# The two middle column groups of an output projection, computed as one pair of seven block products

## The chip, the cores and the metric

The kernel runs on one core of a Trainium2 chip. The metric is the device time of one execution, in microseconds (us); lower is better. Engines are named as in the profile: PE is TensorE (matmuls; PEld are its weight loads), DVE is VectorE, ACT is ScalarE, POOL is GpSimd and SP is SyncE, which here only issues transfers.

## The reference

Two layers of a decoder trunk, 512 tokens by 2048 channels in float32. Each layer normalises its input, projects it to 6656 columns, runs three token mixers on parts of these (retention with 6 heads, differential attention with 4 heads, a gated linear recurrence, called LRU, on 768 channels), joins their gated outputs to 2048 channels, and sends these through one output projection:

```python
mixed = jnp.concatenate([ret_out, diff_out, lru_out], axis=-1)
y = jnp.einsum('bse,ed->bsd', mixed, w_out[l])
x = x + rms_norm(y, post_norm_g[l])
```

The change concerns the second of these lines: a product of a 512x2048 matrix (`mixed`) with a 2048x2048 matrix (`w_out`), once for each layer.

## The kernel before

**Precision.** Each float32 operand of a projection is split in two parts, `hi` (rounded to the type fp32r) and `lo` (what is left), and each product is made of three matmuls: hi by hi, hi by lo and lo by hi (L204). Weights are split when they are loaded: ScalarE writes `whi` (L164), VectorE subtracts it from the raw weights and writes `wlo` (L165). Activations are split where they are produced; for the output projection these are 16 pairs `mhi`, `mlo` of 128 channels by 512 tokens.

**Tiling.** All weights come in chunks of 256 rows by 512 columns (`raw`, 512 KB, two k-tiles of 128 rows). There are three buffers each of `raw`, `whi` and `wlo`. A `Pass` (L89) is one column group of 512 columns: 8 chunks, all 16 k-tiles. `run_pass` (L191) runs over chunks and, in a chunk, over up to four accumulators of 128x512 in PSUM (`big`, four banks). In form B, that of the output projection, the accumulators are the four blocks of 128 tokens, the activations are the stationary operand and 512 columns of weights move. The last two chunks are done bank after bank, so that the banks end one after the other; each bank's `evac` follows when its last matmul is issued.

**The output projection** is four column groups (L899 to L902). The fourth is done in two halves of two token blocks. The order of k-tiles is LRU, retention, differential attention (`outk`, L851), as the mixers end. `evac_y` (L794) takes the sum of squares of a result on ScalarE (L797) and multiplies by the gain of the norm on VectorE (L804); after the fourth group, `finish` (L820) scales, adds the residual, stores, and for layer 0 also transposes and splits the input of layer 1.

**Order of the work.** Loads are asked for by `ensure` (L168) two chunks ahead of the matmuls. The smaller work of the mixers is written as generators in a queue `side`, of which `pump` (L177) advances one step after each second group of matmuls; `drain` empties it before the output projection (L971). Instructions on PE, DVE, ACT and POOL are put in order at build time by a planner with priorities: loads, weight splits and `evac` have a bonus of 300 instructions (`HP`, L43). SP is left in program order (`manual_schedule`, L100), so a transfer that waits for its buffer holds up those behind it. Almost all tiles of 128x512 come from one pool `up` of 77 buffers (`NU`, L37): a new tile waits until a buffer is free. The residual's input tiles `xr` are loaded by `load_x` (L777), started before the third group (L976), two at each step; `finish` needs those of two token blocks after each half of the fourth group.

Of the kernel before, what the change touches and what calls it, by code (L numbers as in the profile page):

```python
# [23 lines left out]
P = 128  # L24
DM = 2048
S = 512
# [11 lines left out]
WBUFS = 3  # L38
NWARM = 9
# [6 lines left out]
C_RQ, C_RV, C_RG, C_DQ, C_DK, C_DV, C_DG, C_LX = 0, 1536, 2304, 3072, 3584, 4096, 4608, 5120  # L46

# [41 lines left out]
class Pass:  # L89
    def __init__(self, form, wsrc, kts, banks, act, evac, defer=False):  # L90
        self.form, self.wsrc, self.kts = form, wsrc, kts
        self.banks, self.act, self.evac, self.defer = banks, act, evac, defer


@with_exitstack
def tile_hybrid_trunk(ctx, tc, x, xt, pos, ppar, lamqk, w_in, gw, w_out, postg, cp, cm, out):
# [54 lines left out]
    loaded = [0]  # L151
    last_copy = [None]

    def load_chunk(i):
        p, c = chunk_list[i]
        raw = wp.tile([P, 2, S], F32, tag="raw", name=nm("raw"))
        hi = wp.tile([P, 2, S], F32R, tag="whi", name=nm("whi"))
        lo = wp.tile([P, 2, S], F32R, tag="wlo", name=nm("wlo"))
        src = p.wsrc[c].rearrange("p (k c) -> p k c", k=2)
        for a, b in (((0, 1), (1, 2)) if i == 0 else ((0, 2),)):  # L160
            if i == 0:
                load_xt(a)
            nc.sync.dma_start(raw[:, a:b, :], src[:, a:b, :])
            last_copy[0] = A.copy(hi[:, a:b, :], raw[:, a:b, :])  # L164
            V.tensor_tensor(lo[:, a:b, :], raw[:, a:b, :], hi[:, a:b, :], op=ALU.subtract)  # L165
# [19 lines left out]
    def drain():  # L185
        while side:
            pump()
# [3 lines left out]
    def run_pass(p):  # L191
# [39 lines left out]
        for c in range(nch):  # L231
            del chunk_tiles[base + c]

# [334 lines left out]
    def diff_final(l, st):  # L568
# [3 lines left out]
        for h in range(DIFF_H):  # L572
            ps = SM("dT")
            for tb in range(NT):
                T.transpose(ps[:, tb * P:(tb + 1) * P], st["dod"][tb][:, h * P:(h + 1) * P], ident)
            hi, lo = U("mhi", F32R), U("mlo", F32R)
            A.activation(hi, ps, AF.Identity, scale=subg[:, l:l + 1])
            V.scalar_tensor_tensor(lo, ps, subg[:, l:l + 1], hi, op0=ALU.mult, op1=ALU.subtract)
            st["mix"][6 + h] = (hi, lo)
            yield  # L580
# [85 lines left out]
    def lru_final(st):  # L666
# [8 lines left out]
        for t in range(LRU_T):  # L675
# [7 lines left out]
            st["mix"][10 + t] = (hi, lo)  # L683
# [56 lines left out]
    def ret_final(st, heads):  # L740
        for h in heads:
# [8 lines left out]
            st["mix"][h] = (hi, lo)  # L750
# [26 lines left out]
    def load_x(l, st):  # L777
        src = x2 if l == 0 else xs
        for tb in range(NT):
            for n in range(4):  # L780
# [3 lines left out]
                if n % 2:  # L784
                    yield
# [8 lines left out]
    def evac_y(l, st, n):  # L794
        def f(tb, ps):
            y = U("y")
            A.activation(junk, ps, AF.Square, accum_out=ssy[:, tb, n:n + 1])  # L797
            st["y"][tb, n] = y
# [5 lines left out]
            V.tensor_tensor(y, ps, st["pg"][n], op=ALU.mult)  # L804
            if n == 2:
# [36 lines left out]
    def new_state():  # L842
        return {k: {} for k in ("h", "dq", "dk", "dqs", "dks", "dv", "dg", "lx", "lg", "lh", "rq", "rk", "rv", "rg", "ro",
                                "mix", "y", "ry", "xr", "pg")} | {"turned": None}
# [6 lines left out]
    outk = list(range(10, 16)) + list(range(0, 10))  # L851
    layer_passes = []
    for l in range(DEPTH):
# [45 lines left out]
        for n in range(4):  # L899
            groups = [tbs] if n < 3 else [[0, 1], [2, 3]]  # L900
            for g in groups:
                seq.append((Pass("B", WO[n], outk, g, st["mix"], evac_y(l, st, n)), []))  # L902
        layer_passes.append(seq)
        for p, _ in seq:
            passes.append(p)
            for c in range(len(p.kts) // 2):
                chunk_list.append((p, c))
# [55 lines left out]
    for l in range(DEPTH):  # L963
# [5 lines left out]
        for i, (p, tasks) in enumerate(layer_passes[l]):  # L969
            if i == 13:  # L970
                drain()  # L971
            if i in (13, 14, 15, 16):
                n = i - 13
# [104 lines left out]
```

## Time and profile before

| | |
|---|---|
| time, median of 3 runs | 1637.45 us (1636.26 to 1637.54) |
| profiled execution | 1638.29 us |
| its span, first to last instruction | 1636.5 us |
| granted TensorE clock | 0.998 |
| PE busy | 1624.9 us, 99% |
| DVE busy | 928.4 us, 57% |
| ACT busy | 646.3 us, 39% |
| POOL busy | 60.1 us, 4% |
| HBM read, written | 167.86 MB, 8.39 MB; 108 GB/s over the span |

The profile is one execution; its time is compared with its own span, and medians with medians. A group of instructions is named by its line, engine, operation, output and inputs (`big<-whi,mhi` is a matmul of the output projection), the count, and then busy time and the mean duration of one in ns. Matmuls are pipelined: the next begins before the one before has ended, so the distance between starts, and not the duration, tells what one costs. "Idle before" is the engine's idle time just ahead of the group's instructions, with what ended it.

### The profile page before, as it was taken

What the parts mean: (1) busy time and instruction counts of PE and PEld (TensorE: products, weight loads), DVE (VectorE), ACT (ScalarE), POOL (GpSimd) and SP (SyncE); (2) the same over time, 40 slices, a digit from 0 to 9 for tenths busy, and PEclk for the clock granted to TensorE, in tenths of its full rate; (3) what the DMA queues carried; (4) which work ended last, traced back from release to release, by engine and by line L of the source; (5) the groups of instructions that cost most, each with busy time, mean ns of one, the idle gap of its engine ahead of it and who ended that gap; (6) DMA issues with size and microseconds to landing.
All of it is one profiled execution on the core that took longest, in us unless ns stands there. A gap on an engine that the chain in (4) does not pass through costs nothing.

```text
span 1636.5 us, 19326 instructions
## 1 busy us (share of the span) xinstructions
PE 1624.9 (99%) x7541; PEld 1344.5 (82%) x7541; DVE 928.4 (57%) x1558; ACT 646.3 (39%) x1014; POOL 60.1 (4%) x84
## 2 busy tenths in 40 slices
PE   9999999999999999999999999999999999999997
PEld 7888888888788888888888888887888888888886
DVE  7657756556586555233762774645857644442336
ACT  7243334346742223222752343435673222332232
POOL 1010000000000000000120000000000000000001
PEclk9999999999999999999999999999999999999999
DMA  6423331323233222354643223222323322233635
GB/s 229 124 86 108 97 96 59 98 78 98 79 102 95 79 72 85 109 173 137 217 155 103 91 91 102 65 85 79 100 87 91 102 65 78 90 99 107 204 124 199
DMA packets 54747, 177.50 MB, mean 108 GB/s; under 512 B 6656, under 2 KB 7680, under 8 KB 54656
## 3 DMA queue, kind: packets, MB, share of 16 engines
q1 hardware_dynamic: 52592, 169.94, 32.4%
q0 software_dynamic: 1920, 6.29, 1.1%
q8 instruction: 59, 0.97, 0.2%
q14 instruction: 32, 0.26, 0.1%
q10 hardware_dynamic: 144, 0.04, 0.0%
HBM read 167.86 MB, written 8.39 MB: 108 GB/s over the span
## 4 chain that ended last, share of the span: by engine, by line
PE 83%; issue 14%; DVE 1%; ACT 1%; DMA 0%; POOL 0%; POOLq 0%; DVEq 0%; ACTq 0%
PE big L209 75%; PE gate L622 1%; PE acc L515 1%; PE rs L691 1%; PE ro L716 1%; PE sc L482 1%; PE sc L483 1%; DVE wlo L165 1%; PE wT L505 1%; PE ro L719 0%; PE kv L705 0%; PE hT L831 0%; DVE y L823 0%; DMA raw<-in_w_out 0%; ACT whi L164 0%
## 5 line engine op out<-in xcount | busy, mean ns | idle before, releaser
L165 DVE TENSOR_TENSOR wlo<-raw,whi 128x1024 fp32r<-128x1024 f32 (+1 forms) x289 | 351.3, 1219 | 440.7 <-ACT whi L164 423.1
L164 ACT CAST whi<-raw 128x1024 fp32r<-128x1024 f32 (+1 forms) x289 | 302.4, 1048 | 590.9 <-PE big L209 477.1
L209 PE MATMUL big<-hhi,whi 128*128 128x512 f32 x1024 | 401.8, 393 | 0.0
L209 PE MATMUL big<-hhi,wlo 128*128 128x512 f32 x1024 | 399.1, 390 | 0.0
L209 PE MATMUL big<-hlo,whi 128*128 128x512 f32 x1024 | 399.0, 390 | 0.0
L209 PE MATMUL big<-whi,hhi 128*128 128x512 f32 x640 | 254.4, 400 | 0.0
L209 PE MATMUL big<-whi,hlo 128*128 128x512 f32 x640 | 250.8, 392 | 0.0
L209 PE MATMUL big<-wlo,hhi 128*128 128x512 f32 x640 | 250.2, 392 | 0.0
L209 PEld LDWEIGHTS big<-hhi,wlo 128*128 128x128 f32 x1024 | 192.2, 188 | 40.6
L209 PEld LDWEIGHTS big<-hhi,whi 128*128 128x128 f32 x1024 | 192.4, 188 | 39.5
L209 PEld LDWEIGHTS big<-hlo,whi 128*128 128x128 f32 x1024 | 192.4, 188 | 38.7
L209 PE MATMUL big<-whi,mhi 128*128 128x512 f32 x512 | 199.9, 390 | 0.4 <-ACT whi L164 0.4
L209 PE MATMUL big<-wlo,mhi 128*128 128x512 f32 x512 | 199.4, 390 | 0.5 <-DVE wlo L165 0.5
L209 PE MATMUL big<-whi,mlo 128*128 128x512 f32 x512 | 199.8, 390 | 0.0
L209 PEld LDWEIGHTS big<-wlo,hhi 128*128 128x128 f32 x640 | 120.7, 189 | 26.0
L209 PEld LDWEIGHTS big<-whi,hhi 128*128 128x128 f32 x640 | 121.0, 189 | 24.3 <-ACT whi L164 0.8
L209 PEld LDWEIGHTS big<-whi,hlo 128*128 128x128 f32 x640 | 120.9, 189 | 23.7
L209 PEld LDWEIGHTS big<-wlo,mhi 128*128 128x128 f32 x512 | 96.1, 188 | 20.8 <-DVE wlo L165 1.0
L209 PEld LDWEIGHTS big<-whi,mhi 128*128 128x128 f32 x512 | 96.1, 188 | 20.6 <-ACT whi L164 0.9
L209 PEld LDWEIGHTS big<-whi,mlo 128*128 128x128 f32 x512 | 96.1, 188 | 19.6
L491 ACT ACTIVATE pr<-sc,mx 128x128 f32<-128x128 f32 (+3 forms) x64 | 33.2, 523 | 86.7 <-DVE mx L488 86.7
L417 DVE TENSOR_TENSOR rt<-qk,sin_d 32x512 f32<-32x512 f32 x64 | 43.7, 683 | 3.5 <-ACT qk L459 2.5
(212 smaller groups left out, 1333.1 us busy)
## 6 DMA issues: line engine op xcount, KB each, us to landing
raw<-in_w_in SPq DMA_DIRECT2D x207, 512.0 KB, 3.6
raw<-in_w_out SPq DMA_DIRECT2D x80, 512.0 KB, 3.4
xT<-in_xt SPq DMA_DIRECT2D x16, 256.0 KB, 6.6
xr<-in_x SPq DMA_DIRECT2D x16, 256.0 KB, 6.5
xs<-y POOLq DMA_DIRECT2D x16, 256.0 KB, 3.6
xr<-xs SPq DMA_DIRECT2D x16, 256.0 KB, 5.6
pg<-in_postg SPq DMA_DIRECT2D x8, 256.0 KB, 3.8
out<-y POOLq DMA_DIRECT2D x8, 256.0 KB, 5.9
```

The lines of the kernel that those rows point to most:

```text
L164: last_copy[0] = A.copy(hi[:, a:b, :], raw[:, a:b, :])
L165: V.tensor_tensor(lo[:, a:b, :], raw[:, a:b, :], hi[:, a:b, :], op=ALU.subtract)
L209: T.matmul(ps[b], lhsT=lhsT, rhs=rhs, start=(cnt[b] == 0), stop=(cnt[b] == total - 1))
L417: V.tensor_tensor(t2[b:b + w, :], raw[a:a + w, :], sin[a:a + w, :], op=ALU.mult)
L482: T.matmul(ps[:, :n], lhsT=qs[:, blk], rhs=ks[:, :n], start=True, stop=False)
L483: T.matmul(ps[:, :n], lhsT=qs[:, blk], rhs=kl[:, :n], start=False, stop=True)
L491: A.activation(p[:, :n], sc[c][:, :n], AF.Exp, bias=mx[:, c:c + 1], scale=0.125, accum_out=sums[:, h:h + 1])
L505: T.transpose(ps[:, kb * P:(kb + 1) * P], w[:, kb * P:(kb + 1) * P], ident)
L515: T.matmul(accs[i][:, h * P:(h + 1) * P], lhsT=wt[:, kb * P:(kb + 1) * P], rhs=dv[kb][:, h * P:(h + 1) * P], start=(kb == 0), stop=(kb == i))
L622: T.matmul(ps[:BW, :], lhsT=wt[:BW, cols], rhs=at[:BW, :], start=(n == 0), stop=(n == 2))
L691: T.matmul(ps[:, n * P:(n + 1) * P], lhsT=k[:, n * P:(n + 1) * P], rhs=q[:, n * P:(n + 1) * P], start=True, stop=True)
L716: T.matmul(po[:, n * P:(n + 1) * P], lhsT=sT[:, n * P:(n + 1) * P], rhs=v[:, n * P:(n + 1) * P], start=True, stop=(n == 0))
```

## The change

The first and the fourth column group stay plain. The second and the third become one `Pair`, a product of block matrices two by two: the activations are halved by tokens (256 and 256) and by channels (k-tiles 0 to 7 and 8 to 15), the weights by channels and by columns (512 and 512). In place of eight block products seven are made, of sums and differences of blocks (Winograd's form). One product is a 256x1024 by 1024x512 matrix product: four units, one for each weight chunk, of 12 matmuls (two token blocks, two k-tiles, three matmuls). The order of units is A11 B11 alone, and then three couples that alternate unit by unit: S1 T1 with S3 T3, S2 T2 with S4 B22, A12 B21 with A22 T4. A unit keeps two accumulators open for four units, so a couple fills the four banks.

- **Sums of activations** (S1 to S4): the class `Sums` makes them on VectorE while the first group runs, and splits them in hi and lo; they stay in the pool `up`. The splits of the fourth are made later, from the second S1 unit on. It works on unsplit activations `mf`, which `diff_final` and `ret_final` now copy from PSUM with one more ScalarE instruction each (ten a layer); for LRU they are put together again as hi + lo. All activations are also renumbered so that k-tiles 0 to 5 are LRU's (`K_LRU`, `K_RET`, `K_DIFF`); the order of the weight rows was this before.
- **Sums of weights** (T1, T2, T4) are made on VectorE in a tile pair `x` in `up`, to which the chunk just loaded is added; T3 is made by a transfer from POOL's queue that adds the second chunk to a loaded one (`accum_op`). Chunks of the lower right block are so read twice.
- **Loading in three steps**: `ensure` now loads a pair's chunk four units before it is split, adds two units before, and splits as before. Plain chunks are loaded and split at the last step.
- **Results**: products A11 B11, S1 T1 and S3 T3 are copied from PSUM to `up` by ScalarE (`held`); the others are combined with these by VectorE. The squares and the gain are then taken from SBUF, in place. The mean square is closed when the three first groups of a token block are there, whichever ends last.
- `load_x` is started at the first unit of A12 B21 and loads one tile for each step.

```diff
+A11_B11, A12_B21, S1_T1, S2_T2, S4_B22, S3_T3, A22_T4 = range(7)
+SUM_OF = {S1_T1: 0, S2_T2: 1, S3_T3: 2, S4_B22: 3}
+UNITS = [(A11_B11, c) for c in range(4)] + [
+    (s, c) for both in ((S1_T1, S3_T3), (S2_T2, S4_B22), (A12_B21, A22_T4)) for c in range(4) for s in both]
...
+    def load_unit(i):
+        p, (s, c) = chunk_list[i]
+        w1, w2 = p.w
+        if s == A11_B11:
+            src = p.x[c] = [U("wx"), U("wx")]
+            for kk in range(2):
+                nc.sync.dma_start(src[kk], w1[c][:, kk * S:(kk + 1) * S])
+        elif s == S1_T1:
+            p.kept[c] = load_raw(w2[c])
+        elif s == S2_T2:
+            p.kept[c] = load_raw(w2[c + 4])
+        elif s == A12_B21:
+            p.kept[c] = load_raw(w1[c + 4])
+        yield
+        if s in (S1_T1, S2_T2, A22_T4):
+            src = p.x[c]
+            for kk in range(2):
+                V.tensor_tensor(src[kk], src[kk], p.kept[c][:, kk, :], op=ALU.add)
+        elif s != A11_B11:
+            src = p.kept[c]
+        if s == S3_T3:
+            nc.gpsimd.dma_start(src, w2[c + 4].rearrange("p (k c) -> p k c", k=2), accum_op=ALU.add)
+        yield
+        hi, lo = split_tiles()
+        if isinstance(src, list):
+            for kk in range(2):
+                split(hi[:, kk, :], lo[:, kk, :], src[kk])
+        else:
+            split(hi, lo, src)
+        chunk_tiles[i] = (hi, lo)
+        yield
     def ensure(i):
-        while loaded[0] <= min(i, len(chunk_list) - 1):
-            with tc.high_priority(HP):
-                load_chunk(loaded[0])
-            loaded[0] += 1
+        for step, more in enumerate((LOAD, ADD, 0)):
+            while loaded[step] <= min(i + more, len(chunk_list) - 1):
+                n = loaded[step]
+                if n not in steps:
+                    steps[n] = (load_unit if isinstance(chunk_list[n][0], Pair) else load_chunk)(n)
+                with tc.high_priority(HP):
+                    next(steps[n])
+                loaded[step] += 1
...
+    def run_pair(p, begin):
...
+        def evac(s, t, x):
+            o1, o2 = p.out
+            if s in (A11_B11, S1_T1, S3_T3):
+                held = {A11_B11: p1, S1_T1: p5, S3_T3: p7}[s]
+                held[t] = U("held")
+                A.copy(held[t], x)
+            elif s == A12_B21:
+                e = U("e")
+                V.tensor_tensor(e, x, p1[t], op=ALU.add)
+                o1(t, e)
+            elif s == S2_T2:
+                w, e = U("w"), U("e")
+                V.tensor_tensor(w, x, p1[t], op=ALU.subtract)
+                V.tensor_tensor(p5[t], p5[t], w, op=ALU.add)
+                V.tensor_tensor(e, p5[t], p7[t], op=ALU.subtract)
+                V.tensor_tensor(p7[t], p7[t], w, op=ALU.subtract)
+                o2(2 + t, e)
+            elif s == S4_B22:
+                V.tensor_tensor(p5[t], x, p5[t], op=ALU.add)
+                o2(t, p5.pop(t))
+            else:
+                V.tensor_tensor(p7[t], x, p7[t], op=ALU.add)
+                o1(2 + t, p7.pop(t))
+
+        for n, (s, c) in enumerate(UNITS):
+            if (s, c) in begin:
+                side.append(begin[s, c]())
+            if s in SUM_OF:
+                until(lambda: (SUM_OF[s], c) in p.sums.parts)
+            ensure(base + n + 2)
+            hi, lo = chunk_tiles.pop(base + n)
+            for t in range(2):
+                if c == 0:
+                    ps[s, t] = pb.tile([P, S], F32, tag="big", name=nm("big"))
+                for kk in range(2):
+                    ah, al = (stationary(s, c, kk, part)[:, t * P:(t + 1) * P] for part in range(2))
+                    for m, (wt, at) in enumerate(((hi, ah), (hi, al), (lo, ah))):
+                        T.matmul(ps[s, t], lhsT=at, rhs=wt[:, kk, :], start=(c == kk == m == 0),
+                                 stop=(c == 3 and kk == 1 and m == 2))
+                if c == 3:
+                    with tc.high_priority(HP):
+                        evac(s, t, ps.pop((s, t)))
+            pump()
+    class Sums:
...
+        def make(self, c):
+            f, plain = self.f, self.plain
+            for k in (2 * c, 2 * c + 1):
+                if k not in f:
+                    f[k] = U("mf")
+                    hi, lo = self.act[k]
+                    V.tensor_tensor(f[k], hi.bitcast(F32), lo.bitcast(F32), op=ALU.add)
+            yield
+            last = None
+            for n in (0, 2, 1, 3):
+                t = plain[n, c] = U("sf")
+                for kk in range(2):
...
+                    V.tensor_tensor(t[:, cols], a, b, op=ALU.subtract)
+                if last is not None:
+                    self.split(last, c)
+                last = n
+                if n in (2, 1):
+                    yield
...
+            m = st["mf"][K_RET + h] = U("mf")
+            A.copy(m, ps)
...
-        for n in range(4):
-            groups = [tbs] if n < 3 else [[0, 1], [2, 3]]
-            for g in groups:
-                seq.append((Pass("B", WO[n], outk, g, st["mix"], evac_y(l, st, n)), []))
+        st["sums"] = Sums(st["mf"], st["mix"])
+        seq.append((Pass("B", WO[0], allk, tbs, st["mix"], out_y(l, st, 0)), []))
+        seq.append((Pair(WO[1], WO[2], st["mix"], st["sums"], out_y(l, st, 1), out_y(l, st, 2)), []))
+        for g in ([0, 1], [2, 3]):
+            seq.append((Pass("B", WO[3], allk, g, st["mix"], out_y(l, st, 3)), []))
...
-            if i == 15:
-                side.append(load_x(l, st))
-            run_pass(p)
+            if isinstance(p, Pair):
+                run_pair(p, {(S1_T1, 1): st["sums"].rest, (A12_B21, 0): lambda l=l, st=st: load_x(l, st)})
+            else:
+                run_pass(p)
```

More of the change, by code (lines that the diff above doesn't have):

```diff
@@ L38 @@
 WBUFS = 3
+ADD, LOAD = 2, 4
 NWARM = 9
@@ L150, in tile_hybrid_trunk, with load_raw, split_tiles, split @@
     chunk_tiles = {}
-    loaded = [0]
+    steps = {}
+    loaded = [0, 0, 0]
     last_copy = [None]
+    def load_raw(src):
+        raw = wp.tile([P, 2, S], F32, tag="raw", name=nm("raw"))
+        nc.sync.dma_start(raw, src.rearrange("p (k c) -> p k c", k=2))
+        return raw
+    def split_tiles():
+        return (wp.tile([P, 2, S], F32R, tag="whi", name=nm("whi")),
+                wp.tile([P, 2, S], F32R, tag="wlo", name=nm("wlo")))
+    def split(hi, lo, raw):
+        last_copy[0] = A.copy(hi, raw)
+        V.tensor_tensor(lo, raw, hi, op=ALU.subtract)
@@ L154, in load_chunk @@
     def load_chunk(i):
         p, c = chunk_list[i]
[L156 to L161, printed above, removed]
+        yield
+        yield
+        if i:
+            raw = load_raw(p.wsrc[c])
+            hi, lo = split_tiles()
+            split(hi, lo, raw)
+        else:
+            src = p.wsrc[0].rearrange("p (k c) -> p k c", k=2)
+            raw = wp.tile([P, 2, S], F32, tag="raw", name=nm("raw"))
+            hi, lo = split_tiles()
+            for a in range(2):
@@ L186, in drain, with until @@
         while side:
+            pump()
+    def until(done):
+        while not done():
+            assert side
             pump()
@@ L792, in squares, with out_y, f @@
                     yield
[L794 to L798, printed above, removed]
+    def out_y(l, st, n):
+        def f(tb, src):
+            A.activation(junk, src, AF.Square, accum_out=ssy[:, tb, n:n + 1])
+            y = st["y"][tb, n] = U("y") if n in (0, 3) else src
             if n == 3:
@@ L803, in f @@
                 G.tensor_tensor(st["ry"][tb], ms, mhalf[:, :1], op=ALU.pow)
-            V.tensor_tensor(y, ps, st["pg"][n], op=ALU.mult)
-            if n == 2:
+            V.tensor_tensor(y, src, st["pg"][n], op=ALU.mult)
+            if n < 3 and all((tb, m) in st["y"] for m in range(3)):
                 ss = tiny("sy", 1)
@@ L905, in tile_hybrid_trunk @@
             passes.append(p)
-            for c in range(len(p.kts) // 2):
-                chunk_list.append((p, c))
+            for u in UNITS if isinstance(p, Pair) else range(len(p.kts) // 2):
+                chunk_list.append((p, u))
     st = states[0]
@@ L971, in tile_hybrid_trunk @@
                 drain()
-            if i in (13, 14, 15, 16):
-                n = i - 13
+                side.append(st["sums"].all())
+            for n in {13: (0,), 14: (1, 2), 15: (3,)}.get(i, ()):
                 st["pg"][n] = U("pg")
                 nc.sync.dma_start(st["pg"][n], postg[l, n * S:(n + 1) * S].partition_broadcast(P))
-            if i == 15:
-                side.append(load_x(l, st))
-            run_pass(p)
+            if isinstance(p, Pair):
+                run_pair(p, {(S1_T1, 1): st["sums"].rest, (A12_B21, 0): lambda l=l, st=st: load_x(l, st)})
+            else:
+                run_pass(p)
             for t in tasks:
```

60 lines of the change are left out of this document (50 added, 10 removed).

## The prediction, made before the changed kernel was run

> **What bounds the kernel now.** First the page: busy time by engine, the costliest groups and the issues.
>
> ```profile
> PE 1624.9 (99%) x7541; PEld 1344.5 (82%) x7541; DVE 928.4 (57%) x1558; ACT 646.3 (39%) x1014; POOL 60.1 (4%) x84
> ...
> L209 PE MATMUL big<-whi,mhi 128*128 128x512 f32 x512 | 199.9, 390 | 0.4 <-ACT whi L164 0.4
> ...
> raw<-in_w_out SPq DMA_DIRECT2D x80, 512.0 KB, 3.4
> ...
> out<-y POOLq DMA_DIRECT2D x8, 256.0 KB, 5.9
> ```
>
> TensorE is busy for 99% of the span. The group is one of three of the output projections (512 each, 1536 in all), and it waited 0.4 us in the whole run. A duration of 390 ns is no price, because matmuls overlap; that comes from the chain of waits, which merges runs of matmuls without a gap:
>
> ```profile
> 1.39 4.02 PE warm L953 x9
> ...
> 643.42 145.34 PE big L209 x641
> ```
>
> 145.34 / 641 = 0.2267 us for each matmul, through nearly the whole output projection of layer 0. The stages (engine sums over windows that I laid at 192 x 0.2267 = 43.5 us; columns: PE, PEld, DVE, ACT, POOL busy, granted clock, DMA share, GB/s) are the first, second and third column group, the fourth's first half, then the second and third of layer 1:
>
> ```profile
> 641.10:684.60 43.50, 43.50 (x197) 36.00 (x196) 14.50 (x15) 13.39 (x19) 0.00 (x0) 1.00 0.30 99
> 684.60:728.10 43.50, 43.50 (x194) 36.02 (x193) 12.54 (x13) 11.06 (x17) 0.00 (x0) 1.00 0.49 151
> 728.10:771.60 43.50, 43.50 (x194) 36.02 (x193) 13.20 (x19) 11.06 (x17) 0.00 (x0) 1.00 0.45 151
> 771.60:793.40 21.80, 21.59 (x98) 17.65 (x97) 12.32 (x16) 9.26 (x12) 1.82 (x3) 1.00 0.57 181
> 1495.10:1538.70 43.60, 43.60 (x194) 36.12 (x193) 12.65 (x13) 11.16 (x17) 0.00 (x0) 1.00 0.46 151
> 1538.70:1582.20 43.50, 43.50 (x194) 36.02 (x193) 12.98 (x18) 11.06 (x17) 0.00 (x0) 1.00 0.45 152
> ```
>
> In the stages that the change rewrites, TensorE has no gap at full clock, VectorE is used for 30%, ScalarE for 25%, the DMA engines for under half. A matmul less is worth its 0.2267 us there, as long as the idle engines can carry what replaces it.
>
> **The change, part by part.** *Matmuls removed.* Two plain groups take 2 groups x 16 k-tiles x 4 token blocks x 3 = 384 matmuls in each layer. The pair takes 28 units x 2 halves x 2 k-tiles x 3 = 336, of the same form (a 128x128 stationary, 512 columns moving). 48 less in each layer, 96 in all: 96 x 0.2267 = **21.8 us**. The pair has 336 x 0.2267 = 76.2 us in each layer, a unit of 12 matmuls 2.72 us.
>
> *Work added on VectorE and ScalarE.* Prices come from these groups:
>
> ```profile
> L165 DVE TENSOR_TENSOR wlo<-raw,whi 128x1024 fp32r<-128x1024 f32 x287 | 350.0, 1223 | 440.6 <-ACT whi L164 423.1 <-DMA xr<-in_x 7.6 <-DMA xr<-xs 7.6
> L164 ACT CAST whi<-raw 128x1024 fp32r<-128x1024 f32 x287 | 301.2, 1051 | 590.5 <-PE big L209 477.1 <-issue 95.8 <-DMA raw<-in_w_out 4.6
> ...
> L804 DVE TENSOR_TENSOR y<-big,pg 128x512 f32<-128x512 f32 x32 | 22.1, 689 | 32.2 <-ACT junk L797 31.8
> ...
> L839 DVE SCALAR_TENSOR_TENSOR hlo<-hT,pp,hhi 128x128 fp32r<-128x128 f32 x64 | 19.6, 344 | 2.7 <-ACT hhi L838 2.3
> ...
> L748 ACT CAST mhi<-rT 128x512 fp32r<-128x512 f32 x12 | 7.0, 583 | 11.1 <-PE rT L746 11.1
> ```
>
> An operation on 128x512 is 0.69 us on VectorE and 0.58 on ScalarE, one on 128x1024 1.22 and 1.05. The sums of 256 columns have no row; between 0.344 (128 columns) and 0.689 (512), a third of the way, is 0.46. In the first group's 43.5 us the activation sums add to VectorE 6 x 0.69 (the LRU tiles put together again) + 32 x 0.46 + 12 x 0.69 = 27.1 us, to 14.5 now: 41.6 of 43.5, and the first sum is used only 10.9 us later, after the four units of plain products. It fits, narrowly, so I cost it at nothing; without cover it would be up to 27 us in each layer. In the pair VectorE has 12 whole weight splits (14.6), 16 in halves (32 x 0.69 = 22.1), 24 weight additions (16.6), four late splits (2.8), 14 combinations of products (9.7) and 8 multiplications by the gain (5.5): 71.3 of 76.2 us. On average it is hidden, with 6% to spare; ScalarE, at about 28 x 1.1 + 18 x 0.6 = 42 us, is far from it. The ten extra ScalarE copies of the activations per layer (0.6 us each) lie beside matmuls of the last input projection, where nothing waits for them before the second sums.
>
> *Where the average doesn't hold.* Combinations come in a burst at the end of the second couple (S2 with T2, S4 with B22). How closely VectorE operations follow each other is in its order of time, independent ones first, then a chain in which each needs the one before:
>
> ```profile
> 858.16 0.69 DVE L400 TENSOR_TENSOR cos_d<-cos_d,rsb 128x512 f32<-128x512 f32 x1
> 858.76 0.68 DVE L400 TENSOR_TENSOR sin_d<-sin_d,rsb 128x512 f32<-128x512 f32 x1
> ...
> 72.89 4.32 DVE L259 SCALAR_TENSOR_TENSOR ang<-turn,ang 128x512 f32<-128x512 f32 x6
> ```
>
> Independent ones start 0.60 us apart, dependent ones 4.32 / 6 = 0.72. Count from the start of S2's last unit: its halves end at 1.36 and 2.72, those of S4 at 4.08 and 5.44, and A22's first unit is due at 8.16. That unit accumulates in the bank that S4's first half leaves, and needs its own split weights. Ahead of that bank's release VectorE has, in order of readiness: from 1.3 the split for A12 (1.14 until the next can start), 8 operations for S2's halves, 2 gain products, 2 half splits for A22, and the addition that reads S4's bank. 1.3 + 1.14 + 13 x 0.60 = 10.2, 2.1 us late; with 0.72, 1.3 + 1.22 + 13 x 0.72 = 11.9, 3.7 us late. Below, the planner may take S4's addition first, and nothing is late. I take 2.5, since the halves' chains alternate: **5.0 us** for both layers, bounds 0 to 7.4. Later units find their splits in time again (1.9 us of work on average for each 2.72). The Trainium skill ("VectorE: DVE Perf Modes", section "The DRAIN you can't avoid") says that an operation does not start until the pipe of the one before is empty; by that the step would be the whole 0.69, the unit 3.3 us late and the sum 1.6 us worse; the 0.60 above disagrees for independent operations, and the row decides.
>
> *The accumulating transfer.* Four per layer and 512 KB each, issued on POOL, which has nothing else in these stages (0.00 above). No row has one. The nearest are plain loads in these stages:
>
> ```profile
> DMA to landing us min/median/max: 3.1/3.3/7.9
> ```
>
> From below it is the 3.3 us of a plain load; from above, reading and writing its target as well, twice the longest, 15.8. I take 6, nearest to POOL's store of 256 KB (5.9). A weight buffer holds a load (3.3), two additions (1.4), the transfer, a cast and a subtraction (2.3): 7.0 + L. Three buffers, one couple of units each 5.44 us, give 16.3: free up to L = 9.3. Above it each of the 4 couples per layer loses (L - 9.3) / 3. The second reading of these weights adds 2.1 MB to a stage whose DMA share is 0.45 to 0.49: nothing.
>
> *SyncE's queue.* The pair's loads are issued four units ahead. The input tiles for the residual now come one for each step from the third couple on, the last eight during the fourth group's first half. The load there may land within 3 x 2.72 - 2.3 = 5.9 us of its buffer's release without delay; beside such tiles (16 in 20 us) it took now
>
> ```profile
> raw<-in_w_out SPq DMA_DIRECT2D x4, 512.0 KB, 6.0
> ```
>
> and they come slower here, one for each 2.72 us: 0, bound above (7.9 - 5.9) / 3 x 8 = 5 us per layer.
>
> *Sum.* The profiled execution is 1638.29 us (span 1636.5 and 1.8 around it): 1638.29 - 21.8 + 5.0 = 1621.5. It lies 0.84 above the median of 1637.45, so against the median 1620.7; I say **1621**.
>
> **Rivals.** (a) *All covered*: S4's addition goes first and no unit is late. 1637.45 - 21.8 = 1615.7. For it: the group of output projection matmuls above waited 0.4 us in all. Against: 13 operations in 6 us. (b) *A restart*: if A22 is late by 3.7 us, TensorE comes back slow. The nine matmuls after its first idle time took 4.02 / 9 = 0.447 us each, 0.22 over the rate of later ones (they are bf16, also 512 columns): 2.0 us in each layer. 1637.45 - 21.8 + 2 x (3.7 + 2.0) = 1627. The Trainium skill ("TensorE: Matmul & The Clock Gate", "Part 1: The HAM clock gate") has the clock halved after about 3.4 us of idling; the granted clock of the stages is 1.00 throughout, and no gap of that length is in the trace between its ends. (c) *A slow accumulation*: with L = 13, in the upper half of its bounds, (13 - 9.3) / 3 x 8 = 9.9 us on top: 1631. At 15.8 it is 17 and the gain is gone. For it: nothing shows its rate. (d) *On the other side, the pool of 77 tiles*: I count near the pair's start 32 mixed activations, 24 split sums and 4 plain ones, 8 weight tiles, 4 results, 2 gains and 2 held products: 76. The new weight tiles are loaded by SyncE in order, ahead of the first group's last plain loads. If the last of them waits for a slot until VectorE is through with the sums (41.6 us into the group), the eighth chunk lands at 45.0 and is split at 47.3, while TensorE wants it at 34 (six chunks of 5.44 and half a chunk's matmuls of the first bank): 13.3 us idle per layer, 1621 + 26.6 = 1648. It decides from 8.2 us per layer, a wait until 36.5 us into the group. Against: half of the sums do not exist yet when these tiles are asked for, so some 60 of the 77 are in use.
>
> **How the numbers follow.** Forecast 0.52 (own range 1617 to 1625), (a) 0.18, (b) 0.07, (c) 0.13, (d) 0.10. The range from 1615 to 1630 takes in the forecast, (a), (b) and the milder half of (c), 0.83. No change means within 0.2%, 3.3 us, about what this measurement tells apart. Faster holds the forecast, (a), (b) and nearly all of (c): 0.88. Same is 0.03, the upper end of (c). Slower is (d) without its mild end, 0.09.
>
> **What would show it.** 336 matmuls in each pair at 0.2267 us; one gap of 2 to 3 us for each layer, put down to VectorE, ahead of the third couple's second unit and none of 1 us elsewhere; VectorE above 80% busy in pair and first group; accumulations landing in 4 to 9 us; the first group still 43.5 us. Wrong it is if gaps recur in every couple of S1 and S3 (the transfer), if the first group grows (sums or slots), or if VectorE's operations cost more than 0.69 beside POOL's issuing.

## The result, and the profile after

The kernel after takes 1645.94 us (median of 4 runs, 1645.53 to 1647.76), the one before 1637.49 us beside it (4 runs, 1636.26 to 1638.07). The ratio is 1.0053, with a 95% interval of 1.0041 to 1.0064: **slower by 8.5 us**, where 16 us less were forecast. The profiled execution of after took 1647.76 us, its span is 1646.0 us.

Busy time and the group of plain output matmuls, from the page of after:

```profile
PE 1613.4 (98%) x7445; PEld 1326.6 (81%) x7445; DVE 1048.5 (64%) x1798; ACT 710.4 (43%) x1134; POOL 66.2 (4%) x92
...
L296 PE MATMUL big<-whi,mhi 128*128 128x512 f32 x256 | 102.4, 401 | 6.7 <-ACT whi L190 6.7
```

The saving is there: 7541 - 7445 = 96 matmuls less, 11.5 us less busy time on TensorE. But this group, which had waited 0.4 us, now waits 6.7. What TensorE waited for in the whole run, the five largest rows (`hT` are the transpositions of `finish`; columns: total, times, longest):

```profile
PE big L296 <- ACT whi L190: 6.7, 3, 3.7
PE hT L1024 <- DVE hlo L1032: 5.4, 3, 2.7
PE big L370 <- DVE wlo L191: 3.3, 6, 1.1
PE big L296 <- DVE wlo L191: 3.2, 3, 2.2
PE big L370 <- DVE held L351: 2.1, 2, 1.0
```

The pair's matmuls are L370: 5.4 of these 20.7 us. The larger part, L296 and L1024, is in the two column groups that stayed plain. The stages show the same (columns: PE, PEld, DVE, ACT, POOL busy, clock, DMA share, GB/s; rows: first group, pair and fourth group of layer 0, the same three of layer 1; the windows are laid by eye, that of the pair runs a little over it on both sides, and that of the fourth group begins in its second half and reaches beyond it):

```profile
641.10:684.60 43.50, 41.48 (x183) 33.44 (x182) 33.48 (x63) 20.29 (x33) 1.07 (x1) 1.00 0.31 93
684.60:770.10 85.50, 82.24 (x356) 65.74 (x354) 67.28 (x107) 44.42 (x75) 2.63 (x3) 1.00 0.50 151
797.00:850.00 53.00, 43.66 (x194) 34.46 (x194) 36.09 (x81) 35.50 (x94) 9.95 (x18) 0.87 0.53 179
1465.00:1508.50 43.50, 41.47 (x183) 33.45 (x182) 33.48 (x63) 20.21 (x33) 0.95 (x1) 1.00 0.31 94
1508.50:1593.00 84.50, 81.70 (x354) 65.69 (x353) 66.67 (x106) 43.81 (x74) 2.61 (x3) 1.00 0.53 153
1593.00:1646.00 53.00, 42.72 (x179) 34.22 (x177) 31.08 (x39) 16.66 (x22) 6.71 (x12) 0.92 0.67 228
```

Busy time hides part of a loss: a matmul at a lower clock counts as busy. So I measure a stage's **lost time** from the starts of matmuls: of each distance between two starts, what it has over 0.2267 us, where that is 0.1 us or more. A stage runs from its first matmul to the first of the next stage; before the change, the second and third group stand for the pair. Summed, in us, in the two kernels and three that come below (the sums are of unrounded values):

| lost time | before | after | x_two | mf_parts | x_two_mf |
|---|---|---|---|---|---|
| first group, both layers | 0 | 5.4 | 5.5 | 0 | 0 |
| pair, both layers | 0 | 8.9 | 7.0 | 7.1 | 7.2 |
| fourth group, layer 0 | 0.4 | 14.2 | 1.0 | 13.2 | 0.9 |
| fourth group, layer 1 | 1.5 | 4.3 | 1.2 | 4.6 | 1.0 |
| sum | 1.9 | 32.8 | 14.7 | 25.0 | 9.0 |

After against before: 32.8 - 1.9 - 21.8 = +9.1 us; the spans differ by 1646.0 - 1636.5 = 9.5. The 0.4 us that are left lie outside these stages or in distances too small for the sum. The table is of one profiled execution of each kernel; that of after is the slowest of its four, so differences from it come out larger than those of the medians (for x_two 18.8 us of span against 14.4).

**The fourth group of layer 0** lost most. TensorE's order of time there:

```profile
799.02 0.66 PE L1024 MATMUL hT<-cmt,held 128*128 128x128 f32 x4 [1.97 <-DVE hlo L1032]
800.41 0.66 PE L1024 MATMUL hT<-cmt,y 128*128 128x128 f32 x4 [0.73 <-DVE hlo L1032]
803.78 1.12 PE L1024 MATMUL hT<-cmt,y 128*128 128x128 f32 x4 [2.71 <-DVE hlo L1032]
808.64 0.79 PE L296 MATMUL big<-whi,mhi 128*128 128x512 f32 x1 [3.75 <-ACT whi L190]
...
813.05 0.63 PE L296 MATMUL big<-whi,mhi 128*128 128x512 f32 x1
813.48 0.63 PE L296 MATMUL big<-whi,mlo 128*128 128x512 f32 x1
...
815.12 0.39 PE L296 MATMUL big<-wlo,mhi 128*128 128x512 f32 x1
```

The projection's matmuls are out of weights: between two batches of transpositions of `finish` there is nothing to run, until `whi` arrives at 808.64. The 14 distances that follow are mostly of 0.427 us in place of 0.2267: 815.12 - 808.64 - 14 x 0.2267 = 3.3 us more. The weights were late because they were asked for late. SyncE's order of time, and what it waited for longest in that stretch besides its weight buffers:

```profile
781.52 0.33 SPq L182 DMA_DIRECT2D raw<-in_w_out  x1
781.90 15.97 SPq L977 DMA_DIRECT2D xr<-in_x  x2
797.99 14.48 SPq L182 DMA_DIRECT2D raw<-in_w_out  x6
```

```profile
SPq L977 <- DVE hlo L1032: 15.4, 1, 15.4
```

One of the last residual tiles `xr` waits 15.4 us for a slot of the pool, and the slot is freed by `hlo`, that is by `finish` of the fourth group's first half itself. The weight loads stand behind it in SyncE's program order from 781.90 to 797.99. The first of them then took 7.1 us to land, at 805.09, and its cast came 2.5 us later still, since operations `hhi` of `finish` stand ahead of it in ScalarE's order:

```profile
807.55 2.92 ACT L190 CAST whi<-raw 128x1024 fp32r<-128x1024 f32 x3
```

In the kernel before, the row of that stretch has no `xr`, and weights are asked for without a break:

```profile
771.86 31.96 SPq L163 DMA_DIRECT2D raw<-in_w_out  x12
```

**The fourth group of layer 1** lost 2.8 us more than before. Here no residual tile waits for a slot (0.4 us at most); a weight load lands late, and ScalarE stands in front of it:

```profile
1619.05 1.05 ACT L190 CAST whi<-raw 128x1024 fp32r<-128x1024 f32 x1 [2.80 <-DMA raw<-in_w_out]
```

**The first group** lost 2.7 us in each layer, nearly all of it some 12 us after its start. ScalarE in time, of after and then of before:

```profile
641.14 0.69 ACT L771 ACTIVATE mf<-dT,subg 128x512 f32<-128x512 f32 x1 [0.82 <-DVE mlo L769]
641.72 0.68 ACT L768 ACTIVATE mhi<-dT,subg 128x512 fp32r<-128x512 f32 x1
643.22 0.69 ACT L771 ACTIVATE mf<-dT,subg 128x512 f32<-128x512 f32 x1 [0.82 <-DVE mlo L769]
...
649.26 1.29 ACT L386 CAST sh<-sf 128x512 fp32r<-128x512 f32 x2 [1.19 <-DVE sf L406]
650.46 1.04 ACT L190 CAST whi<-raw 128x1024 fp32r<-128x1024 f32 x1
```

```profile
641.18 1.84 ACT L577 ACTIVATE mhi<-dT,subg 128x512 fp32r<-128x512 f32 x3 [1.93 <-PE dT L575]
643.46 0.69 ACT L577 ACTIVATE mhi<-dT,subg 128x512 fp32r<-128x512 f32 x1 [0.43 <-PE dT L575]
644.04 1.04 ACT L164 CAST whi<-raw 128x1024 fp32r<-128x1024 f32 x1
```

Before, the four heads' `mhi` run 0.6 us apart and the next weights are cast at 644.04. After, each head goes `mhi`, `mlo` (VectorE), `mf`, 2.08 us a head, a split of the sums comes next, and the cast is at 650.46; a matmul waits 1.49 us for it.

**The pair** lost 4.7 us in layer 0 and 4.2 in layer 1. VectorE's order of time around the predicted turn:

```profile
737.50 1.29 DVE L230 TENSOR_TENSOR wx<-wx,raw 128x512 f32<-128x512 f32 x2 [3.21 <-DMA raw<-in_w_out]
...
746.52 0.68 DVE L347 TENSOR_TENSOR e<-held,held 128x512 f32<-128x512 f32 x1
747.12 0.68 DVE L351 TENSOR_TENSOR held<-big,held 128x512 f32<-128x512 f32 x1
```

It runs without a pause from 737.50 on, one operation each 0.60 us. S4's addition (L351), which frees the bank for A22's first unit, starts at 747.12, and the unit is 1.2 us late. The burst itself began late: its first addition waited 3.21 us for a load, with the next splits behind it, and the matmul that needed the first of these was 1.25 us late.

The accumulating transfers (L234) landed in

```profile
DMA to landing us min/median/max: 5.3/6.1/8.8
```

One of them in each layer came late all the same, because it began late. SyncE's order of time, its longest wait in the first group besides weight buffers, and ScalarE at the second unit of S3 T3:

```profile
686.61 1.53 SPq L1168 DMA_DIRECT2D pg<-in_postg  x2
688.23 21.06 SPq L182 DMA_DIRECT2D raw<-in_w_out  x5
```

```profile
SPq L1168 <- DVE sl L387: 21.4, 1, 21.4
```

```profile
703.08 1.05 ACT L190 CAST whi<-raw 128x1024 fp32r<-128x1024 f32 x1 [4.63 <-DMA raw<-in_w_out]
```

SyncE stood for 21.4 us in front of a gain tile `pg` of the pair, until a split of the activation sums (`sl`) freed a slot of the pool, and the pair's next weight loads went out from 688.23 on, behind it. The transfer that adds to one of these chunks was issued at 697.38, ScalarE waited 4.63 us for it, and in its unit the first matmul that needs `wlo` started 0.7 us late, at 705.45. Layer 1 has the same wait of 21.4 us and a gap at the same unit. With the longer distances beside them these gaps cost 0.9 and 0.6 us. That they come from `pg` is read from the traces; no run takes that wait away.

### The profile page after: what moved, and what is told of

Its sections match the earlier page's. It is cut to its first block, busy times and chain, and to the rows that moved or that the text cites. A ratio compares the mean times of both kernels' runs of the same rounds, so it can differ in the third digit from the quotient of the medians.

```text
span 1646.0 us, 19583 instructions
## 1 busy us (share of the span) xinstructions
PE 1613.4 (98%) x7445; PEld 1326.6 (81%) x7445; DVE 1048.5 (64%) x1798; ACT 710.4 (43%) x1134; POOL 66.2 (4%) x92
## 4 chain that ended last, share of the span: by engine, by line
PE 87%; DVE 6%; issue 3%; DMA 2%; ACT 2%; POOL 0%; DVEq 0%; POOLq 0%; ACTq 0%
PE big L296 75%; PE big L370 4%; DMA raw<-in_w_out 2%; DVE wlo L191 2%; PE gate L815 1%; PE acc L706 1%; ACT whi L190 1%; PE ro L909 1%; PE rs L884 1%; PE sc L673 1%; PE sc L674 1%; PE wT L696 1%; PE ro L912 0%; PE kv L898 0%; DVE wx L230 0%
## 5 line engine op out<-in xcount | busy, mean ns | idle before, releaser
L191 DVE TENSOR_TENSOR wlo<-raw,whi 128x1024 fp32r<-128x1024 f32 (+1 forms) x281 | 340.6, 1218 | 320.1 <-ACT whi L190 315.5
L190 ACT CAST whi<-raw 128x1024 fp32r<-128x1024 f32 (+1 forms) x281 | 293.2, 1047 | 485.3 <-PE big L296 319.1
L296 PE MATMUL big<-hhi,whi 128*128 128x512 f32 x1024 | 401.8, 393 | 0.0
L296 PE MATMUL big<-hhi,wlo 128*128 128x512 f32 x1024 | 399.1, 390 | 0.0
L296 PE MATMUL big<-hlo,whi 128*128 128x512 f32 x1024 | 398.9, 390 | 0.0
L296 PE MATMUL big<-whi,hhi 128*128 128x512 f32 x640 | 253.3, 398 | 0.0
L296 PE MATMUL big<-whi,hlo 128*128 128x512 f32 x640 | 249.9, 390 | 0.0
L296 PE MATMUL big<-wlo,hhi 128*128 128x512 f32 x640 | 249.8, 391 | 0.0
L296 PEld LDWEIGHTS big<-hhi,wlo 128*128 128x128 f32 x1024 | 192.2, 188 | 40.5
L296 PEld LDWEIGHTS big<-hhi,whi 128*128 128x128 f32 x1024 | 192.5, 188 | 39.4
L296 PEld LDWEIGHTS big<-hlo,whi 128*128 128x128 f32 x1024 | 192.4, 188 | 38.8
L296 PEld LDWEIGHTS big<-wlo,hhi 128*128 128x128 f32 x640 | 120.2, 188 | 26.2 <-DVE wlo L191 0.5
L296 PEld LDWEIGHTS big<-whi,hhi 128*128 128x128 f32 x640 | 120.5, 188 | 24.1 <-ACT whi L190 1.0
L296 PEld LDWEIGHTS big<-whi,hlo 128*128 128x128 f32 x640 | 120.5, 188 | 23.8
L296 PE MATMUL big<-whi,mhi 128*128 128x512 f32 x256 | 102.4, 401 | 6.7 <-ACT whi L190 6.7
L296 PE MATMUL big<-wlo,mhi 128*128 128x512 f32 x256 | 100.6, 400 | 3.4 <-DVE wlo L191 3.2
L296 PE MATMUL big<-whi,mlo 128*128 128x512 f32 x256 | 101.2, 396 | 0.0
L296 PEld LDWEIGHTS big<-whi,mhi 128*128 128x128 f32 x256 | 49.1, 192 | 18.1 <-ACT whi L190 8.5
L296 PEld LDWEIGHTS big<-wlo,mhi 128*128 128x128 f32 x256 | 49.3, 192 | 16.6 <-DVE wlo L191 6.3
L296 PEld LDWEIGHTS big<-whi,mlo 128*128 128x128 f32 x256 | 49.1, 192 | 9.9
L370 PE MATMUL big<-wlo,sh 128*128 128x512 f32 x128 | 50.5, 395 | 3.3 <-DVE wlo L191 3.3
```

The source lines that it names most:

```text
L190: last_copy[0] = A.copy(hi, raw)
L191: V.tensor_tensor(lo, raw, hi, op=ALU.subtract)
L296: T.matmul(ps[b], lhsT=lhsT, rhs=rhs, start=(cnt[b] == 0), stop=(cnt[b] == total - 1))
L370: T.matmul(ps[s, t], lhsT=at, rhs=wt[:, kk, :], start=(c == kk == m == 0), stop=(c == 3 and kk == 1 and m == 2))
```

## The experiments

Theory: the residual tiles in SyncE's queue cost some 15 us and the unsplit copies `mf` some 5 us, both outside the pair; the pair itself works nearly as forecast. The "before" beside each is 1637.46 to 1637.76 us.

**x_two: two residual tiles for each step again.**

```diff
                 st["xr"][tb, n] = t
-                yield
+                if n % 2:
+                    yield
```

> The changed kernel with one part undone: the residual's input tiles are asked for two at each step again, still from A12 B21's first unit on. Theory (SyncE's queue): the last two of layer 0's tiles wait 16 us for a slot in the pool of 77 and hold up the plain loads behind them; asked for earlier they find slots, the gaps of 14.6 us in the fourth group go, and 2 us at the end of layer 1 with them: 1645.9 - 16.6 = 1629, between 1627 and 1633. Rival (the closing work on VectorE and ScalarE, which also put the next layer's input in order, is too much for the half group, whatever is loaded): the gaps stay, 1643 to 1648.

Measured 1631.54 us (4 runs, 1628.96 to 1632.13), ratio 0.9960 (0.9946 to 0.9975). Fourteen us from this one edit. The tiles are now all asked for by 756, none waits over 1 us, and the weights follow at once:

```profile
740.84 8.44 SPq L977 DMA_DIRECT2D xr<-in_x  x12
...
755.31 0.86 SPq L977 DMA_DIRECT2D xr<-in_x  x2
...
758.43 40.91 SPq L182 DMA_DIRECT2D raw<-in_w_out  x14
```

In the table above the two rows of the fourth group fall from 14.2 and 4.3 us to 1.0 and 1.2; the first group keeps its loss, and the pair changes by 1.9. So the tiles are a cause by themselves, and not the copies by another way.

**mf_parts: no unsplit copies of the differential heads.** The sums of these are made on VectorE from hi and lo, as for LRU.

```diff
-            m = st["mf"][K_DIFF + h] = U("mf")
-            A.activation(m, ps, AF.Identity, scale=subg[:, l:l + 1])
...
-            for k in (2 * c, 2 * c + 1):
+            for k in (2 * c, 2 * c + 1, 2 * c + 8, 2 * c + 9):
```

> The changed kernel without the four unsplit copies that ScalarE takes of the differential heads' PSUM banks in each layer; the sums put these activations together again from hi and lo on VectorE (4 x 0.69 us more in the first group). Theory: the copies tie ScalarE and VectorE into a chain of 2.1 us per head, behind which the weight splits of the first group's second chunk wait; without them the gap of 2.35 us in each layer goes: 1645.9 - 4.7 = 1641. Rival (the casts for the sums, not the copies, hold the splits up, or VectorE is too full): within 1.5 us of 1645.9, or slower.

Measured 1640.27 us (10 runs), ratio 1.0015 (1.0006 to 1.0025): 5.7 less than after. The first group's lost time goes to 0, the fourth's stays. VectorE's extra work is hidden there, the copies on ScalarE were not.

**x_two_mf: both.**

> Both of the two edits before: residual tiles two at each step, and no unsplit copies of the differential heads. If the two causes are separate their gains add: 1645.9 - 16.6 - 4.7 = 1625. What is left above the 1616 of a full cover is then the pair's own gaps, 4 us per layer. If the queue is not the cause: 1641.

Measured 1623.30 us (1621.99 to 1624.29), ratio 0.9913 (0.9898 to 0.9927): **14.5 us quicker than the kernel before** (1637.76), and 22.6 quicker than after. Each edit alone gave 14.4 and 5.7, which is 20.1; the 2.5 us between are about the width of the intervals. Its account closes: 9.0 - 1.9 - 21.8 = -14.7, and the span is 1622.0, 14.5 less than before's.

**x_pool: the same transfers from POOL's queue.**

```diff
-                nc.sync.dma_start(t, src[tb * P:(tb + 1) * P, n * S:(n + 1) * S])
+                nc.gpsimd.dma_start(t, src[tb * P:(tb + 1) * P, n * S:(n + 1) * S])
```

> The changed kernel with the residual's input tiles at the same points of the program, one at each step, but issued from POOL's queue. The tiles get their slots as late as before, but SyncE's loads no longer stand behind them. Theory (the order in SyncE's queue is what costs): most of the 14.6 us in the fourth group go, 1630 to 1635. Rivals: if the tiles' own lateness costs (the closing work waits for them) or the closing work is too much, 1642 to 1648.

Measured 1638.72 us (10 runs; one of them took 4185.97 us, for which nothing here gives a reason), ratio 1.0005 (0.9995 to 1.0015). That lies between the theory's range and that of the rivals. The fourth groups lose 0.8 and 1.9 us, but the pair loses 17.8 us in both layers in place of 8.9:

```profile
PE big L370 <- DVE wlo L191: 9.9, 8, 2.1
```

POOL's instructions are put in order by the planner, and it put nearly all of the tiles early: POOL issues 15 of them from 713.41 to 742, beside the pair's own loads, and the additions in VectorE's order wait for these (726.60, 3.53 us for `raw`). So the tiles were asked for early, as in x_two, and this run does not tell the queue from the time of asking. That the weight loads stood behind the tiles is shown by SyncE's order of time in after.

**x_early_mf: one tile for each step, but begun earlier,** at the first unit of S2 T2 (with no `mf` copies).

```diff
-                run_pair(p, {(S1_T1, 1): st["sums"].rest, (A12_B21, 0): lambda l=l, st=st: load_x(l, st)})
+                run_pair(p, {(S1_T1, 1): st["sums"].rest, (S2_T2, 0): lambda l=l, st=st: load_x(l, st)})
```

> As mf_parts (1640.3), the residual's tiles still one at each step but begun at the first unit of S2 T2, eight units earlier, so that all have been asked for by the end of the pair. Theory (what matters is that none is asked for once the closing work of the fourth group takes the slots): as with two at each step, 1623, at most 3 us more if some wait for slots in the pair. Rival (one for each step between plain loads is what hurts): 1632 to 1640.

Measured 1624.21 us (1622.88 to 1625.26), ratio 0.9918 (0.9901 to 0.9934), as with two for each step. When the last tiles are asked for decides, not how many come at a step.

**plain_late: the kernel before, with only the asking for residual tiles made late.** There is no pair here.

```diff
-                if n % 2:
-                    yield
+                yield
...
-                side.append(load_x(l, st))
+                side.append(chain(lead(8), load_x(l, st)))
```

> This is the kernel before, with four plain column groups and no pair, in which only the residual's input tiles are asked for differently: one tile for each step in place of two, and from eight steps into the third group on, so that the last eight are asked for during the first half of the fourth group, as in the kernel after. Nothing is left out. Theory (SyncE's in-order queue: the last of these tiles wait for slots of the pool that the last phase of the layer holds, and the weight loads stand behind them; the pair itself has no part in it): matmuls wait in the fourth group of layer 0 as in the kernel after, 10 to 14 us with the slow matmuls that follow, and 1 to 3 us at the end of layer 1; time 1637.5 + 11 to 17 = 1648 to 1654 us, and the profile shows a transfer of this kind waiting over 10 us for VectorE's hlo. Rival (it takes the pair's own tiles in the pool, its held results and sums, to make the slots short): the plain kernel has slots to spare, the tiles are loaded when asked for, time within 2 us of 1637.5.

Measured 1652.64 us (1652.20 to 1655.25), ratio 1.0095 (1.0080 to 1.0110): 14.9 us slower than the kernel before (1637.74), from this alone. What SyncE and TensorE waited for:

```profile
SPq L782 <- DVE hlo L838: 17.0, 1, 17.0
```

```profile
PE hT L830 <- DVE hlo L838: 5.4, 3, 2.7
PE big L209 <- ACT whi L164: 3.7, 1, 3.7
PE big L209 <- DVE wlo L165: 2.1, 1, 2.1
```

The same three waits in the same places, to a tenth of a us, without any of the pair's tiles in the pool. It is the fourth group's own `finish` that holds the slots, and the pair is not needed for it.

**The rest in the pair.** Four edits of x_two_mf went after the 7.2 us that the pair still loses. *act_evac*: ScalarE copies the products of S2 and S4 out of PSUM first, so that banks don't wait for VectorE. *add1*: weight sums are added one unit ahead of the split in place of two. *act_add1*: both. *free_first*: the two operations that free a bank go first in VectorE's order.

act_evac:

```diff
+                A.copy(w, x)
-                V.tensor_tensor(w, x, p1[t], op=ALU.subtract)
+                V.tensor_tensor(w, w, p1[t], op=ALU.subtract)
...
+                b = U("held")
+                A.copy(b, x)
-                V.tensor_tensor(p5[t], x, p5[t], op=ALU.add)
+                V.tensor_tensor(p5[t], b, p5[t], op=ALU.add)
```

add1:

```diff
-ADD, LOAD = 2, 4
+ADD, LOAD = 1, 4
```

free_first:

```diff
+                with tc.high_priority(FREE):
+                    V.tensor_tensor(w, x, p1[t], op=ALU.subtract)
...
+                with tc.high_priority(FREE):
+                    V.tensor_tensor(p5[t], x, p5[t], op=ALU.add)
```

> As x_two_mf (1623.3, with both causes of the loss taken away), and S2 T2 and S4 B22 are copied from PSUM by ScalarE too, so that their banks come free without VectorE; VectorE's combinations then read SBUF. Theory (the turn to the third couple waits for banks behind VectorE's burst): the two waits of 0.34 and 1.04 us in each layer go, with what follows them 1.5 us: 1623.3 - 3 = 1620. Rival (VectorE's backlog as such is late, and the same unit would then wait for its split weights): within 1 us of 1623.

> As x_two_mf, but weight sums are asked for one unit ahead of the split, not two. Theory: VectorE stands 3.6 us in front of an addition whose chunk has not landed, with the ready split of the unit before behind it in its queue; asked for later, it no longer does, and the gap of 1.9 us at the end of layer 0's second couple goes: 1621. Rival: the accumulating transfer has a unit less of time, 6.1 us from issue to landing as it has, and units of S3 T3 begin to wait: 1624 to 1632.

> Both edits before on x_two_mf. If both theories hold 1618, 2 us above the 1616 that the removed matmuls would give with everything covered; if neither, 1623.

> The quicker kernel of these runs (two residual tiles for each step, no unsplit copies of the differential heads) with one more change, in the order of VectorE's work alone: the two operations that free an accumulator at the turn to the third couple, the subtraction that reads S2's product and the addition that reads S4's, get a bonus of 100 instructions in the planner over the other combinations. By that the addition that reads S4's first product stands fifth behind the first subtraction of S2 in place of tenth. Nothing is left out. Theory (the gap of 1.2 us at A22's first unit is this addition standing behind operations that free no bank; the number of operations in the burst matters less than its order): that gap closes in both layers and what was behind is late nowhere else, time 1623.3 - 2.4 = 1621 us. Rival (VectorE is short of time there in sum, so the wait goes to the split of the next weights): a gap of 1 us before wlo or e takes its place, time within 1 us of 1623.3.

| | us | ratio (95% interval) |
|---|---|---|
| x_two_mf | 1623.30 | 0.9913 (0.9898 to 0.9927) |
| act_evac | 1625.51 | 0.9923 (0.9908 to 0.9938) |
| add1 | 1623.77 | 0.9916 (0.9901 to 0.9931) |
| act_add1 | 1624.51 | 0.9918 (0.9903 to 0.9933) |
| free_first | 1624.25 | 0.9913 (0.9899 to 0.9926) |

None gains, where 2 to 5 us were expected each time. Waits of the pair's matmuls in x_two_mf, act_evac and free_first, in this order:

```profile
PE big L370 <- DVE wlo L191: 2.7, 3, 1.7
PE big L370 <- DVE held L351: 2.1, 2, 1.0
```

```profile
PE big L373 <- DVE wlo L191: 3.5, 5, 1.1
PE big L373 <- ACT held L353: 1.0, 2, 0.5
```

```profile
PE big L373 <- DVE wlo L192: 4.7, 8, 1.8
```

In free_first the addition did move from the tenth to the fifth place behind the first subtraction, and the wait for `held` is gone. But the split of A22's weights now stands behind it, and the gaps at the turn of layer 0 come to 1.8 us in place of 1.9. The wait changes its name, not its length.

In add1 the theory was hardly put to the test, for the addition still stands in the same place, with the same splits behind it (x_two_mf had 3.63 us here):

```profile
734.11 1.30 DVE L230 TENSOR_TENSOR wx<-wx,raw 128x512 f32<-128x512 f32 x2 [2.84 <-DMA raw<-in_w_out]
```

The gap that was to go fell from 1.9 to 1.2 us, and layer 1 got one of 1.1 us at another unit of its second couple. In the other edits this wait is 2.84 to 3.64 us.

**gain_out: less work in the burst.** x_two_mf without the multiplications by the gain for the third column group.

```diff
-            V.tensor_tensor(y, src, st["pg"][n], op=ALU.mult)
+            if n != 2:
+                V.tensor_tensor(y, src, st["pg"][n], op=ALU.mult)
```

> The quicker kernel of these runs (two residual tiles for each step, no unsplit copies of the differential heads), which leaves out the four multiplications by the gain for the third column group, all of which lie in the burst of operations at the turn to the third couple; the output lacks that gain. Theory (the two gaps of about 1.2 us and 0.4 us at that turn are VectorE's backlog of about 13 operations of 0.6 us): four operations less take up to 2.4 us from the backlog, both gaps at the turn close in both layers, time 1623.3 - 3 = 1620 us. Rival (what is late there is the order that was written at build time: the operation that frees the bank stays behind the splits and the other results, or the wait goes to the next split): the gap at the turn stays over 0.8 us or another of its size takes its place, time within 1 us of 1623.3.

Measured 1621.39 us (1621.18 to 1622.37), ratio 0.9900 (0.9884 to 0.9917), 1.9 less than x_two_mf, with overlapping intervals. The gap at the turn stays 1.06 us, which is the rival's mark; the pair's waits for VectorE fall by 1.0 us in all (`wlo` 2.7 to 2.0, `held` 2.1 to 1.8). It lies between the two. Only one of the four multiplications had stood ahead of S4's first addition, so the run took little from what that gap waits for. Together with free_first it speaks for the sum of the work in the burst and against its order, but does not settle it.

## Why the prediction was wrong

The forecast of 1621 us was 24.9 us too low. The residual's tiles account for 14.4 of these (x_two), the copies for 5.7 (mf_parts) and the pair's gaps for 3.9 (8.9 against 5.0).

*The matmuls removed*: right. 96 less at 0.2267 us, and x_two_mf's span closes with these 21.8 us.

*SyncE's queue, costed at 0 with a bound of 5 us for each layer*: **the step that failed.** It asked only how long a load takes to land beside residual tiles. It never asked when a residual tile gets its slot, though I had noted that the last eight are asked for during the fourth group's first half and that a transfer waiting for its buffer holds up those behind it. That wait was 15.4 us, in layer 0, and the fourth group lost 14.2 - 0.4 = 13.8 us more than before there. In layer 1 no tile waited for a slot; the 2.8 us lost are a load that landed late, within the bound of 5. x_two took 14.4 us off the time. Rival (d) had the mechanism in kind, a SyncE transfer that waits for a slot ahead of weight loads, and a time of 1648 against the 1645.94 measured. But it put it on the pair's weight tiles in the first group, and there no matmul waited for a late load in either layer; it was near by its number, by luck, and not by its place. plain_late shows that the loss in the fourth group needs no pair. What spoke against (d), some 60 of 77 tiles in use, was wrong: the pool was full in the first group, and a gain tile waited 21.4 us for a slot ahead of the pair's loads. It cost little there, one late unit of S3 T3 in each layer.

*The ten extra ScalarE copies, costed at nothing because "nothing waits for them"*: wrong by 5.7 us (mf_parts). I named matmuls of the input projection as their cover and priced only their consumers. The last four lie at the projection's end, on the engine that must next cast the first group's weights, and each delays the next head's `mhi`, too.

*The first group's sums at nothing*: right; VectorE was 33.48 us busy of 43.5 (41.6 forecast), and without the `mf` copies that group loses 0.

*The pair's work on VectorE, 71.3 of 76.2 us, and the turn at 2.5 us for each layer*: right in kind. VectorE was 67.28 us busy in the pair's window of 85.5, which is under the forecast: I priced each operation of 128x512 at its duration of 0.69 us, and in a run they start 0.60 apart. The turn took 0.5 + 1.2 us, less than 2.5; but gaps of 0.4 to 1.25 us elsewhere, of which I had said that none of 1 us would occur, bring the pair to 8.9 us in both layers against 5.0 forecast and 7.4 as its bound. The largest term not in the sum was an addition that waits for its load (3.21 us) at the head of VectorE's order with splits behind it.

*The accumulating transfer at 6 us, free up to 9.3*: its size was right, 6.1 median and 8.8 at most, so rival (c) is out. But "free" took for granted that it can begin in time, and the one issued at 697.38 did not. *All covered* (a) is out by the pair's 8.9 us.

*A restart* (b): it came, but behind other stalls than the turn: 3.3 us after the gap at 808.64 of layer 0, and 1.7 us (8 distances from 1620.66 to 1624.13) at the end of layer 1. The granted clock of these stages is 0.87 and 0.92. The estimate of 2.0 us for each lies between the two.

What stays open is the pair's last 7.2 us. Five edits leave 1621 to 1626 us. That VectorE has no time to spare in the burst is what free_first and gain_out point to; but in layer 0 it stands idle for 2.8 to 3.6 us just ahead of the burst in all five, in front of the addition whose load is late. A fourth buffer for raw weights, which might let that load start earlier, was not tried, nor were the gain tiles asked for at another place.

## What to carry to other kernels

When a change moves a load in a queue that is kept in program order, ask of each transfer in it two things, when its data are needed and when its buffer is free: a transfer of little use that waits for a slot stops all the weights behind it, and here that cost 14.4 us, as much as the change gained once it was mended (14.5). An instruction that nobody waits for still has a place on its engine; look up what is next there, above all at the seam between two stages. And if the wait changes its name at an edit of the order while the time stays, order alone does not help there: compare the engine's work in that stretch with the time it has, and look at its idle time just ahead of it.

## What was not expected of the hardware

*Slow matmuls after short gaps.* Call a gap what the distance between the starts of two matmuls of 512 columns has over 0.2267 us. Of six gaps of 2.1 to 2.3 us in the traces of all these runs, five were followed within 1.5 us by six or more matmuls 0.427 us apart; gaps of 1.5 to 2.0 us, of which there were a dozen, by none. In x_pool (TensorE's order of time):

```profile
729.09 0.50 PE L370 MATMUL big<-wlo,sh 128*128 128x512 f32 x1 [1.93 <-DVE wlo L191]
...
730.95 0.63 PE L370 MATMUL big<-whi,sl 128*128 128x512 f32 x1
731.38 0.63 PE L370 MATMUL big<-wlo,sh 128*128 128x512 f32 x1
```

The granted clock from 728 to 734 is 0.72. The gap at 743.96 of the same run, 2.24 us, had no such effect. Behind the gap at 729.09 ten distances took 733.07 - 729.09 = 3.98 us, 1.7 us more than 10 x 0.2267: so much a gap of little over 2 us can cost beyond itself. The Trainium skill ("TensorE: Matmul & The Clock Gate", "Part 1: The HAM clock gate") states that the clock is halved after at least one idle window of about 3.4 us. The 0.427 us, twice the quick distance less a little, agrees with the halving; that gaps of 2.1 us were enough does not agree with the length.

*A third reader of a PSUM tile.* `mf` and `mlo` only read the transposed head, yet each `mf` began when `mlo` had ended (0.82 us of idle time in every row), so that a copy of 0.69 us cost 1.5 us a head. Whether the memory or the program's own waits make this order, no run here shows.
